# Regrouping the small matmuls between two recurrence chains of a hybrid attention and RWKV-7 step

## The chip, the cores and the metric

The kernel runs on one core of a Trainium2 chip. Its time is the device time of one execution in microseconds (us); the number that counts is the median over the timed runs. Engines are called as the profile calls them: PE (TensorE matmul), PEld (TensorE weight load), DVE (VectorE), ACT (ScalarE), POOL (GpSimd) and SP (SyncE, which issues the DMAs).

## What is computed

One inference step of a two-layer trunk of width 2048, for 512 latent tokens and 128 context tokens together (640 columns). Layer 0 is attention (differential heads and latent-compressed heads). Layer 1 is RWKV-7 time mixing: 32 heads of 64, one scan forward and one backward over the tokens. Each layer has a modulated norm before it and a gated residual behind it. The part that matters here is the scan of layer 1:

```python
def step(s, inp):
    r_t, w_t, k_t, v_t, kk_t, a_t = inp
    sa = jnp.einsum('bhij,bhj->bhi', s, -kk_t)
    s = s * w_t[:, :, None, :] + sa[..., None] * (kk_t * a_t)[:, :, None, :] + v_t[..., None] * k_t[:, :, None, :]
    return s, jnp.einsum('bhij,bhj->bhi', s, r_t)
```

and the modulation that comes before each norm, `m = silu(cond) @ w + b`, whose weight is 2048 x 6144 per layer.

## The kernel before, in words

All large products are done as three fp32r matmuls (high x high, high x low, low x high part; `project_steps`, L126), 320 columns each, with 128x512 weight tiles that come by DMA (`raw`), are rounded by ACT (`whi`) and subtracted by POOL (`wlo`). In the profile these are the `pj` matmuls (`part` and `first` at the start of the program).

The start of layer 0 (the first 160 us) computes the modulation: `adaln` (L171) reads 128x512 weight tiles (`araw`, 256 KB each) and multiplies them with four 32-column tiles of PE in turn (k = 0, 1, 2, 3, 0, ...; L176). It is a generator that stops after every k; the main code there (JOBS, JW) runs some of its steps, then one job of projection matmuls, and so on, for four blocks b. The order of PE is set by the scheduler there.

Layer 1's scan is done in chunks of 64 tokens. The work is cut in 32 units: 16 tiles of two heads, each in two halves u of five chunks per direction. For each unit the state-independent part is made first: decay and keys (`stage_a1`, `stage_e`: tiles AR and BK), the Gram matrices (`stage_a2`, L1114), the inverse of a unit triangular 64x64 matrix per chunk and head (`stage_a3` on DVE for 16x16 blocks, then `stage_inv` on PE for the rest), transposed keys (`stage_bk`, L1182), transposed values (`stage_pre`, `pvt`, L1202) and a product of Gram matrix and values (`pmv`, L1218). Then `stage_c` runs the chain over five chunks, each step needing the one before, and `stage_gn` normalises its output and transposes it (`pgn`, L1410).

`stage_inv` has four stages on PE with 32x32 tiles of the array, called the first to the fourth stage here: L1243 (result read by DVE at L1246), L1252 (read by DVE at L1257, two transposes, and by ACT at L1259, four copies), L1265 (read by ACT at L1268) and L1272 (read by ACT at L1275). All write the PSUM tile CC. The first two go round four tiles on the diagonal of the array from one matmul to the next. The last two do 20 matmuls on one tile, and then 20 on another.

Inside the scan the order of PE is the order in which the code issues it (`manual_schedule`); each other engine's order is set by the scheduler. `unit(n)` first interleaves the chain of unit n with the plan (P1), then, between this chain and the next, works off the list P2: pairs of a stage and a weight; a step of the stage is issued, and then `fill(weight)` issues projection matmuls from the plan of all coming projections, scaled so that they are spread evenly over the units. What a generator does up to its next `yield` stands on PE in one piece. PSUM tiles of the tag `pg` (two buffers) serve the transposes, `pmv`, and the Gram matrices.

Of the kernel before, what the change touches and what calls it, by code (L numbers as in the profile page):

```python
# [14 lines left out]
AF = mybir.ActivationFunctionType  # L15
# [6 lines left out]
KT = 16  # L22
HT = 320
WC = 512
NCH = 10
# [28 lines left out]
def kernel(  # L54
# [116 lines left out]
    def adaln(layer, psp, tag, sb, sc, blocks, bufs):  # L171
        for n in blocks:
            ps = psp.tile([128, 512], F32, tag=tag, name="ada")
            for k in range(KT):
                j = 32 * (k % 4)
                pe.matmul(ps[j:j + 32, :], sc[:, k, :], ada_raw(layer, n, k, sb, bufs), start=(k < 4),  # L176
                          stop=(k >= 12), tile_position=(0, j))
                yield
            row = sb.tile([128, T], F32, tag="tmp", name="row")[:, 0:512]
            act.activation(out=row, in_=ps, func=AF.Copy)  # L180
            pt = psp.tile([128, 512], F32, tag=tag, name="adat")
            for j in range(4):
                pe.transpose(pt[:, j * 128:(j + 1) * 128], row[:, j * 128:(j + 1) * 128], ident)
            ada_end(layer, n, pt.rearrange("p (j g r) -> p j r g", j=4, g=4)[:, :, 0:2, :], 4)
# [59 lines left out]
    with tc.tile_pool(name="x0", bufs=1, side="right") as xp0, \  # L244
# [42 lines left out]
                else:  # L287
                    dve.tensor_tensor(out=acc if out is None else out, in0=acc, in1=X, op=ALU.add)

        JOBS, JW = (0, 4, 1, 5, 2, 3), (None, (5, 5, 5, 5, 5, 5), (5, 5, 5, 5, 5, 5), (5, 6, 7, 8, 6, 0))  # L290
        for b in range(4):
            ga = adaln(0, pm, "pm", xt0, sc, (b, 4 + b), 8)
            if b:
                for i, job in enumerate(JOBS):
                    for _ in range(JW[b][i]):
                        next(ga, None)
                    if job < 4:
                        part(job, b - 1, None)
                    else:
                        chunk(fg[job - 4])  # L300
            for _ in ga:
                pass
            for k in range(4 * b, 4 * b + 4):
                modulate(x0[:, k, :], 0, k, h0hi, h0lo, xt0)
# [533 lines left out]
    with ExitStack() as l1:  # L838
# [336 lines left out]
        def stage_bk(i, u):  # L1175
            un = units[(i, u)]
            BKn = un.BKn = u1.tile([128, NCH, 128], F32, tag="BKn", name="BKn")
            for c in range(0, NCH, 4):
                n = min(4, NCH - c)
                ps = pg_tile("pbk")  # L1180
                for j in range(n):
                    pe.transpose(ps[:, j * 128:(j + 1) * 128], un.BK[:, c + j, :, :].rearrange("p a t -> p (a t)"), ident)  # L1182
                act.activation(out=BKn[:, c:c + n, :].rearrange("p c d -> p (c d)"), in_=ps[:, 0:n * 128], func=AF.Copy)
                yield

        def stage_v(i, u):
            t, un = tiles_[i], units[(i, u)]
# [7 lines left out]
        def stage_pre(i, u):  # L1195
            un = units[(i, u)]
            vv = un.vv
            UV = un.UV = u1.tile([128, NCH, 128], F32, tag="UV", name="UV")
            for c, n in ((0, 4), (4, 1)):
                ps = pg_tile("pvt")  # L1200
                for j in range(n):
                    pe.transpose(ps[:, j * 128:(j + 1) * 128], vv[:, c + j, :], ident)  # L1202
                for z in range(2):
                    o = 64 * (1 - z)
                    act.activation(out=UV[o:o + 64, un.ca[z] + c:un.ca[z] + c + n, :].rearrange("p c d -> p (c d)"),
                                   in_=ps[o:o + 64, 0:n * 128], func=AF.Copy)
                yield
            MV = un.MV = u1.tile([128, 5, 128], F32, tag="MV", name="MV")
            for s0, n in ((0, 4), (4, 1)):
                ps = pg_tile("pmv")  # L1210
                for s in range(s0, s0 + n):
                    for h in range(2):
                        hs = slice(64 * h, 64 * h + 64)
                        co = 128 * (s - s0) + 64 * h
                        for z in range(2):
                            cg = un.ca[z] + (4 - s if z else s)
                            o, ov = 64 * z, 64 * (1 - z)
                            pe.matmul(ps[o:o + 64, co:co + 64], un.GG[ov:ov + 64, cg, h, 0:64],  # L1218
                                      UV[ov:ov + 64, cg, hs], start=True, stop=True)
                act.activation(out=MV[:, s0:s0 + n, :].rearrange("p c d -> p (c d)"), in_=ps[:, 0:128 * n], func=AF.Copy)  # L1220
                yield

        def stage_inv(i, u):
            un = units[(i, u)]
# [30 lines left out]
            for o, col, q0 in grp:  # L1255
                if col == 0:
                    dve.transpose(out=b2(xn[o:o + 32]), in_=pa(o))  # L1257
            for o, col, q0 in grp:
                act.activation(out=b2(xd[o:o + 32, :, col:col + 32]), in_=pa(o), func=AF.Copy)  # L1259
            yield  # L1260
            t32 = xn
            for z, a, b, ca, cb in zh:
                o = 64 * z
                for q in range(10):
                    pe.matmul(blk(o + 32, q), G[o:o + 32, 2 * ca + q, 32:64], xn[o:o + 32, q, :],  # L1265
                              start=True, stop=True, tile_position=(o, o + 32))
            for o in (0, 64):
                act.activation(out=b2(t32[o + 32:o + 64]), in_=pa(o + 32), func=AF.Copy)  # L1268
            yield
            for o in (0, 64):  # L1270
                for q in range(10):
                    pe.matmul(blk(o, q), t32[o + 32:o + 64, q, :], xd[o + 32:o + 64, q, 32:64],  # L1272
                              start=True, stop=True, tile_position=(o + 32, o))
            for o in (0, 64):
# [111 lines left out]
        def stage_gn(i, u):  # L1386
# [20 lines left out]
            for s0, n in ((0, 4), (4, 1)):  # L1407
# [4 lines left out]
                for z in range(2):  # L1412
# [3 lines left out]
                        act.activation(out=y, in_=p4[:, :, z, :], func=AF.Copy)  # L1416
                    else:
                        dve.tensor_tensor(out=y, in0=y, in1=p4[:, :, z, :], op=ALU.add)
                yield

        def stage_bonus(i, u):
            if u:
# [59 lines left out]
                next(work[0], None)  # L1482

        CW = (3, 3, 2, 3)
        P2 = (('inv', 1), ('bk', 2), ('inv', 2), ('bk', 1), ('pre', 2), ('inv', 2), ('bonus', 1), ('bk', 1), ('inv', 2), ('pre', 2), ('bonus', 2), ('pre', 2), ('pre', 2), ('a2', 3), ('a2', 3), ('a2', 4))
        W2 = sum(w for _, w in P2)

        def step(g):
# [2 lines left out]
        def unit(n):  # L1491
# [5 lines left out]
            sub, a1, kk = of(stage_a3, n + 1), of(stage_a1, n + 2), kk_of(n + 2)  # L1497
            gn = stage_gn(*seq[n - 1]) if n else iter(())
            bonus, inv = of(stage_bonus, n), urgent(of(stage_inv, n + 1))
            P1 = {-1: [kk], 2: [gn, sub, kk], 4: [a1], 5: [kk, sub], 7: [a1], 8: [gn], 10: [a1], 11: [gn], 13: [a1], 15: [bonus]}  # L1500
            w1 = 0
            for g in P1[-1]:
                step(g)
# [25 lines left out]
        def prologue():  # L1529
# [10 lines left out]
                step(g)  # L1540
                fill(w)
            all_(a2, of(stage_a3, 0))
            for g, w in ((bk, 6), (bk, 6), (a1, 8), (bk, 6)):
                step(g)
                fill(w)
            all_(a1, bk)
# [1 line left out]
            all_(of(stage_e, 1))  # L1548
            of(stage_v, 0)
            script(dict(pre=of(stage_pre, 0), inv=urgent(of(stage_inv, 0)), a2=of(stage_a2, 1)),  # L1550
                   (("pre", 6), ("pre", 32), ("inv", 3), ("a2", 6), ("inv", 3), ("inv", 3),
                    ("a2", 6), ("pre", 3), ("inv", 3), ("pre", 3), ("a2", 6)))
            need(proj_r, 1)

        with tc.manual_schedule(engines={mybir.EngineType.PE}):
# [137 lines left out]
```

## Time and profile before

| | |
|---|---|
| median of 3 runs | 3726.73 us (3720.97 to 3733.14) |
| profiled execution | 3717.45 us, of which the span from the first to the last instruction is 3715.7 us |
| PE / DVE / ACT / POOL busy | 94% / 59% / 43% / 32% of the span |
| scan of layer 1 | from about 1640 us to about 3430 us |

Busy time of PE counts matmuls that overlap once. In a timeline row the first number is the start of the first of `x` instructions, the second the time to the end of the last; two rows that follow each other overlap, so that the cost of a group is read from its start to the start of the next row (its pitch). An fp32 matmul is two instructions in the trace and one in the order of the program, an fp32r matmul is one in both.

### The profile page before, as it was taken

To read this page: it belongs to the slowest core of one execution; us is meant where nothing else is said; L and a number is where in the kernel's file an instruction comes from. 1 tells how busy PE (TensorE), PEld (TensorE's weight loads), DVE (VectorE), ACT (ScalarE), POOL (GpSimd) and SP (SyncE) were. 2 spreads that over 40 slices of the span, in tenths; PEclk is the share of its full clock that TensorE was granted. 3 is DMA by queue.
4 is the path that set the end of the run, shared out by engine and by line. 5 is a ranking of instruction groups with operands and counts; after the bars stand their busy time and mean duration, and the time that the engine had idled before them with its cause. 6 is when DMAs were issued, how large, how long until landed. Compare 5 with 4: busy or idle time off the path is not lost. (4 is left out here: it accounts for less than half of the span.)

```text
span 3715.7 us, 83258 instructions
## 1 busy us (share of the span) xinstructions
PE 3491.8 (94%) x34176; PEld 3054.6 (82%) x34176; DVE 2183.1 (59%) x4232; ACT 1608.9 (43%) x3310; POOL 1189.5 (32%) x1094
## 2 busy tenths in 40 slices
PE   7999999999999989999999999999999999999998
PEld 3788889988888889887777787878878878787898
DVE  3355655666667564556666566666666666666402
ACT  2344443444444422544454444444444545445322
POOL 1222112222223344432333332323323333332444
PEclk9999999999999989999999999999999999999999
DMA  8723433333333464322222222222232222223534
GB/s 288 240 80 93 126 100 113 108 102 108 107 108 118 144 204 152 104 77 62 73 62 68 59 65 73 62 65 62 63 76 67 61 67 67 65 68 89 162 101 142
DMA packets 388462, 376.18 MB, mean 101 GB/s; under 512 B 200496, under 2 KB 242416, under 8 KB 388080
## 3 DMA queue, kind: packets, MB, share of 16 engines
q1 hardware_dynamic: 388080, 370.86, 34.3%
q8 instruction: 268, 4.39, 0.5%
q14 instruction: 114, 0.93, 0.1%
HBM read 328.51 MB, written 42.24 MB: 100 GB/s over the span
## 5 line engine op out<-in xcount | busy, mean ns | idle before, releaser
L101 POOL TENSOR_TENSOR wlo<-raw,whi 128x512 fp32r<-128x512 f32 (+1 forms) x628 | 854.4, 1361 | 2032.1 <-PE pj L126 1232.3
L126 PE MATMUL pj<-h0hi,wlo 128*128 128x320 f32 x4448 | 1091.2, 324 | 17.5 <-POOL wlo L101 17.3
L126 PE MATMUL pj<-h0hi,whi 128*128 128x320 f32 x4448 | 1089.2, 324 | 4.8 <-DVE gt L951 3.1
L126 PE MATMUL pj<-h0lo,whi 128*128 128x320 f32 x4448 | 1081.2, 322 | 1.1 <-POOL h0lo L101 0.8
L126 PEld LDWEIGHTS pj<-h0hi,wlo 128*128 128x128 f32 x4448 | 749.6, 192 | 51.9 <-POOL wlo L101 20.7
L126 PEld LDWEIGHTS pj<-h0hi,whi 128*128 128x128 f32 x4448 | 749.2, 192 | 38.3 <-issue 9.1
L126 PEld LDWEIGHTS pj<-h0lo,whi 128*128 128x128 f32 x4448 | 751.8, 191 | 29.2 <-issue 8.0
L100 ACT ACTIVATE whi<-raw 128x512 fp32r<-128x512 f32 (+1 forms) x628 | 390.5, 623 | 734.6 <-PE pj L126 444.0
L198 DVE SCALAR_TENSOR_TENSOR aacc<-araw,scs,aacc 128x512 f32<-128x512 f32 x480 | 401.7, 885 | 20.0 <-DMA araw<-in_dram 19.0
L362 DVE TENSOR_REDUCE nm<-S 128x1 f32<-128x768 f32 (+1 forms) x120 | 98.5, 821 | 257.6 <-PE S L374 257.5
L722 DVE SCALAR_TENSOR_TENSOR x<-pj,mod,xr 128x512 f32<-128x512 f32 (+2 forms) x68 | 33.3, 526 | 251.8 <-PE pj L126 246.1
L365 ACT ACTIVATE P<-S,nm 128x768 f32<-128x768 f32 (+1 forms) x120 | 95.2, 793 | 164.8 <-DVE nm L362 164.3
L1118 DVE TENSOR_TENSOR GG<-gram,con 128x512 f32<-128x512 f32 (+1 forms) x192 | 107.8, 597 | 79.6 <-PE gram L1114 79.5
L1303 ACT ACTIVATE Yn<-CC 128x128 f32<-128x128 f32 x160 | 44.4, 277 | 217.2 <-DVE rhs L1333 209.1
L1114 PE MATMUL gram<-AR,BK 64*128 64x128 f32 x1280 | 115.9, 295 | 20.8 <-DVE GG L1118 13.8
L1114 PEld LDWEIGHTS gram<-AR,BK 64*128 64x128 f32 x1280 | 91.8, 191 | 46.3 <-DVE GG L1118 24.1
L1348 DVE COPY UV<-CC 64x128 f32<-64x128 f32 x160 | 47.1, 295 | 130.6 <-ACT UV L1347 129.2
L1054 PE MATMUL plo<-lr,lw 96*128 96x320 f32 x256 | 104.1, 489 | 6.9 <-DMA lr<-lorad 6.6
L1347 ACT ACTIVATE UV<-CC 64x128 f32<-64x128 f32 x160 | 43.2, 270 | 148.0 <-PE CC L1345 147.4
L564 PE MATMUL po<-PT,vt 128*128 128x128 f32 x800 | 103.2, 276 | 0.1
L564 PEld LDWEIGHTS po<-PT,vt 128*128 128x128 f32 x800 | 98.0, 191 | 4.2 <-issue 2.5
L1056 ACT ACTIVATE tmp<-plo,vecs 128x320 f32<-128x320 f32 x128 | 67.5, 527 | 67.2 <-PE plo L1054 67.2
(338 smaller groups left out, 5306.3 us busy)
## 6 DMA issues: line engine op xcount, KB each, us to landing
raw<-in_dram SPq DMA_DIRECT2D x612, 256.0 KB
araw<-in_dram SPq DMA_DIRECT2D x384, 256.0 KB
lr<-lorad SPq DMA_DIRECT2D x128, 120.0 KB
Ld<-GG SPq DMA_DIRECT2D x64, 160.0 KB
lw<-in_dram SPq DMA_DIRECT2D x128, 48.0 KB
x<-in_dram SPq DMA_DIRECT2D x16, 320.0 KB
xr<-in_dram SPq DMA_DIRECT2D x16, 320.0 KB
DD<-Xd SPq DMA_DIRECT2D x32, 160.0 KB
```

The lines of the kernel that those rows point to most:

```text
L100: act.activation(out=hi, in_=src, func=AF.Copy)
L101: (lo_eng or pool).tensor_tensor(out=lo, in0=src, in1=rf(hi), op=ALU.subtract)
L126: pe.matmul(p[:n, 0:b - a], w, x[:, kk ^ flip, a:b], start=(kk == order[0] and i == 0), stop=(kk == order[-1] + kc - 1 and i == 2))
L198: dve.scalar_tensor_tensor(out=acc[:, s], in0=raw, scalar=scs[:, k, s:s + 1], in1=acc[:, s], op0=ALU.mult, op1=ALU.add)
L362: dve.tensor_reduce(out=nm, in_=S[:, 0:nk], axis=AX.X, op=ALU.max, negate=True)
L365: act.activation(out=P[:, 0:nk], in_=S[:, 0:nk], func=AF.Exp, bias=nm, accum_out=l)
L564: pe.matmul(po[:, 0:128], H.vt[:, kt, :], PT[:, j, :], start=(j == 0), stop=(j == n - 1))
L1054: pe.matmul(ps[:, 0:HT], lw, lo, start=True, stop=True)
L1056: act.activation(out=hv(tmp, z, ca, cb), in_=c3(ps[:, 0:HT]), func=AF.Exp, scale=-1.0, bias=nw0[:, bcol:bcol + 1])
L1114: pe.matmul(ps[:, j * 128:(j + 1) * 128], BK[hs, c + j, :, :].rearrange("p a t -> p (a t)"), AR[hs, c + j, :, :].rearrange("p a t -> p (a ...
L1118: dve.tensor_tensor(out=GG[:, c:c + n, h, :], in0=ps[:, 0:n * 128].rearrange("p (j t) -> p j t", t=128), in1=maskg.rearrange("p (o t) -> p ...
L1348: dve.tensor_copy(out=UV[64:128, cgs[1], :], in_=pu[1][64:128])
```

## The change

Five edits, all on the order of work; no instruction's shape is changed, and no arithmetic.

1. `stage_inv`: in the third and fourth stage the loop over q is outside and the loop over the two tiles inside. Of the four ACT copies behind the second stage (L1259) the two of the off-diagonal column stay; the other two (`xd[o:o+32, :, 0:32]`) are issued behind the third stage.
2. `stage_bk`, `stage_pre`, `stage_gn` yield less often: eight transposes and then two (before 4, 4, 2), five `pvt` (before 4, 1), twenty `pmv` matmuls (before 16, 4), five `pgn` (before 4, 1).
3. P2 puts each of these right behind a stage of the inverse with weight 0 between them; P1 loses one step of `gn`.
4. `adaln` makes four `araw` tiles, then issues four matmuls, then yields; it yields once more behind the ACT copy `row`. It has 12 buffers instead of 8.
5. JW and the weights of the prologue are adapted to the new number of steps.

```diff
-            for k in range(KT):
-                j = 32 * (k % 4)
-                pe.matmul(ps[j:j + 32, :], sc[:, k, :], ada_raw(layer, n, k, sb, bufs), start=(k < 4),
-                          stop=(k >= 12), tile_position=(0, j))
+            for g in range(0, KT, 4):
+                raws = [ada_raw(layer, n, g + j, sb, bufs) for j in range(4)]
+                for j, raw in enumerate(raws):
+                    pe.matmul(ps[32 * j:32 * j + 32, :], sc[:, g + j, :], raw, start=(g == 0),
+                              stop=(g == KT - 4), tile_position=(0, 32 * j))
                 yield
             row = sb.tile([128, T], F32, tag="tmp", name="row")[:, 0:512]
             act.activation(out=row, in_=ps, func=AF.Copy)
+            yield
...
-            ga = adaln(0, pm, "pm", xt0, sc, (b, 4 + b), 8)
+            ga = adaln(0, pm, "pm", xt0, sc, (b, 4 + b), 12)
...
-            for c in range(0, NCH, 4):
-                n = min(4, NCH - c)
+            for c, n in ((0, 4), (4, 4), (8, 2)):
                 ps = pg_tile("pbk")
...
-                yield
+                if c:
+                    yield
...
             for o, col, q0 in grp:
                 if col == 0:
                     dve.transpose(out=b2(xn[o:o + 32]), in_=pa(o))
-            for o, col, q0 in grp:
-                act.activation(out=b2(xd[o:o + 32, :, col:col + 32]), in_=pa(o), func=AF.Copy)
+                else:
+                    act.activation(out=b2(xd[o:o + 32, :, col:col + 32]), in_=pa(o), func=AF.Copy)
             yield
             t32 = xn
-            for z, a, b, ca, cb in zh:
-                o = 64 * z
-                for q in range(10):
+            for q in range(10):
+                for z, a, b, ca, cb in zh:
+                    o = 64 * z
                     pe.matmul(blk(o + 32, q), G[o:o + 32, 2 * ca + q, 32:64], xn[o:o + 32, q, :],
...
+            for o in (0, 64):
+                act.activation(out=b2(xd[o:o + 32, :, 0:32]), in_=pa(o), func=AF.Copy)
             yield
-            for o in (0, 64):
-                for q in range(10):
+            for q in range(10):
+                for o in (0, 64):
                     pe.matmul(blk(o, q), t32[o + 32:o + 64, q, :], xd[o + 32:o + 64, q, 32:64],
...
+        P2 = (('inv', 0), ('bk', 5), ('inv', 0), ('bk', 4), ('inv', 0), ('pre', 5), ('inv', 0), ('pre', 5), ('bonus', 1), ('bonus', 1), ('a2', 4),
+              ('a2', 4), ('a2', 4))
```

On PE, in the 22nd inverse of the program, from its second to its fourth stage, the order before was this (`pj` are projections, `pbn` a small sum over heads):

```order
L1252 MATMUL CC<-DD,t_14641 32x32 x40
L126 MATMUL pj<-h0hi,wlo 128x320 x2
L126 MATMUL pj<-h0hi,whi 128x320 x2
L126 MATMUL pj<-h0lo,whi 128x320 x2
L1182 MATMUL pbk<-con,BK 128x128 x4
L126 MATMUL pj<-h0hi,wlo 128x320 x2
L1202 MATMUL pvt<-con,vv 128x128 x4
L126 MATMUL pj<-h0hi,whi 128x320 x2
L126 MATMUL pj<-h0lo,whi 128x320 x2
L126 MATMUL pj<-h0hi,wlo 128x320 x2
L1265 MATMUL CC<-DD,GG 32x32 x20
```

and it is this now:

```order
L1254 MATMUL CC<-DD,t_14641 32x32 x40
L1183 MATMUL pbk<-con,BK 128x128 x2
L126 MATMUL pj<-h0lo,whi 128x320 x2
L126 MATMUL pj<-h0hi,wlo 128x320 x2
L126 MATMUL pj<-h0hi,whi 128x320 x2
L126 MATMUL pj<-h0lo,whi 128x320 x2
L126 MATMUL pj<-h0hi,wlo 128x320 x2
L1267 MATMUL CC<-DD,GG 32x32 x20
L1204 MATMUL pvt<-con,vv 128x128 x5
```

Between the second and the third stage there were seven pairs of `pj` and eight transposes; now there are five pairs and two transposes, and the `pvt` transposes follow the third stage. From the first stage to the second it goes from four transposes and four pairs to eight transposes and eight pairs; from the third to the fourth seven pairs follow the five `pvt`; behind the fourth the twenty `pmv` follow at once and then eight pairs, and up to the first Gram matrix there are 30 pairs of `pj` instead of 32.

On DVE, at the same place, the order before was this (`AR` and `BK` are made here for the unit after next):

```order
L1246 SCALAR_TENSOR_TENSOR t_14641<-CC,nlow,i_14637 128x5x16 x2
L1087 TENSOR_TENSOR AR<-kk,D 128x5x63
L1090 TENSOR_TENSOR AR<-rT,D 128x5x64
L1087 TENSOR_TENSOR AR<-kk,D 128x5x63
L1090 TENSOR_TENSOR AR<-rT,D 128x5x64
L1397 TENSOR_SCALAR gst<-gst 128x10
L1257 STREAM_TRANSPOSE DD<-CC 32x320 x2
```

and it is this now:

```order
L1248 SCALAR_TENSOR_TENSOR t_14641<-CC,nlow,i_14637 128x5x16 x2
L1089 TENSOR_TENSOR AR<-kk,D 128x5x63
L1092 TENSOR_TENSOR AR<-rT,D 128x5x64
L1089 TENSOR_TENSOR AR<-kk,D 128x5x63
L1092 TENSOR_TENSOR AR<-rT,D 128x5x64
L1259 STREAM_TRANSPOSE DD<-CC 32x320
L1085 TENSOR_TENSOR BK<-kk,az 128x5x64 x2
L1259 STREAM_TRANSPOSE DD<-CC 32x320
```

The two transposes behind the second stage stood together; now two products for BK stand between them. ACT's first copy (L1261) waits for the first transpose, the second transpose for that copy, and ACT's second copy for the second transpose.

## Rows read from the trace of the kernel before

**Rows 1.** The page: busy time of each engine, with share of the span and number of instructions.

```profile
PE 3491.8 (94%) x34176; PEld 3054.6 (82%) x34176; DVE 2183.1 (59%) x4232; ACT 1608.9 (43%) x3310; POOL 1189.5 (32%) x1094
```

**Rows 2.** Busy time by stretch: start and end, length, busy time of PE, PEld, DVE, ACT, POOL with the number of instructions, granted clock of PE, share of the DMA engines, GB/s. The first two are parts of the start, the third is the scan.

```profile
20.00:57.00 37.00, 28.32 (x99) 6.77 (x97) 18.36 (x31) 9.15 (x16) 0.05 (x1) 1.00 0.89 306
57.00:160.00 103.00, 100.80 (x595) 67.31 (x596) 20.44 (x43) 24.85 (x42) 26.66 (x21) 1.00 0.79 264
...
1640.00:3430.00 1790.00, 1678.92 (x22608) 1429.38 (x22608) 1160.39 (x2643) 853.59 (x1880) 567.07 (x630) 0.98 0.26 67
```

**Rows 3.** Whom PE waited for in the scan (1640 to 3430 us): us in total, times, longest.

```profile
PE CC L1265 <- ACT xd L1259: 27.2, 25, 2.6
PE CC L1345 <- ACT Yn L1303: 17.5, 37, 0.8
PE gram L1114 <- DVE GG L1118: 13.8, 18, 3.4
...
PE gram L1114 <- ACT MV L1220: 3.6, 11, 0.9
```

**Rows 4.** PE's timeline in the 22nd inverse, each stage with the row that follows it: start, length, engine, line, names, shapes, number of instructions, idle time before.

```profile
2839.72 0.86 PE L1243 MATMUL CC<-DD,GG 32*32 32x16 f32 x80
2840.51 0.56 PE L126 MATMUL pj<-h0lo,whi 128*128 128x320 f32 x2
...
2842.31 0.89 PE L1252 MATMUL CC<-DD,t 32*32 32x32 f32 x80
2843.13 0.56 PE L126 MATMUL pj<-h0hi,wlo 128*128 128x320 f32 x2
...
2846.84 1.35 PE L1265 MATMUL CC<-DD,GG 32*32 32x32 f32 x40 [0.51 <-ACT xd L1259]
2848.11 0.56 PE L126 MATMUL pj<-h0hi,whi 128*128 128x320 f32 x2
...
2850.79 1.35 PE L1272 MATMUL CC<-xd,DD 32*32 32x32 f32 x40
2852.07 0.56 PE L126 MATMUL pj<-h0hi,whi 128*128 128x320 f32 x2
2852.47 0.46 PE L126 MATMUL pj<-h0lo,whi 128*128 128x320 f32 x2
2852.76 0.46 PE L126 MATMUL pj<-h0hi,wlo 128*128 128x320 f32 x2
2853.06 0.27 PE L1202 MATMUL pvt<-con,vv 128*128 128x128 f32 x1
2853.08 0.54 PE L126 MATMUL pj<-h0hi,whi 128*128 128x320 f32 x2
2853.46 0.46 PE L126 MATMUL pj<-h0lo,whi 128*128 128x320 f32 x2
...
2854.92 0.46 PE L126 MATMUL pj<-h0hi,wlo 128*128 128x320 f32 x2
2855.31 1.15 PE L1218 MATMUL pmv<-UV,GG 64*64 64x64 f32 x32
2856.39 0.55 PE L126 MATMUL pj<-h0hi,whi 128*128 128x320 f32 x2
```

**Rows 5.** PE's timeline a little earlier, in the chain: four `pgn` transposes behind a 64-column group, with the two rows that follow.

```profile
2826.62 0.66 PE L1410 MATMUL pgn<-con,Yn 128*128 128x128 f32 x4
2827.04 0.54 PE L126 MATMUL pj<-h0lo,whi 128*128 128x320 f32 x2
2827.41 0.45 PE L126 MATMUL pj<-h0hi,wlo 128*128 128x320 f32 x2
```

**Rows 6.** The timelines of DVE and ACT behind the second stage of the 22nd inverse.

```profile
2843.89 1.05 DVE L1257 STREAM_TRANSPOSE DD<-CC 32x320 f32<-32x320 f32 x2
2845.03 1.75 ACT L1259 ACTIVATE xd<-CC 32x320 f32<-32x320 f32 x4 [2.49 <-DVE DD L1257]
```

**Rows 7.** Groups of instructions in the scan: line, engine, names, shapes, number | busy us, mean ns of one | idle time of the engine before them, and for whom.

```profile
L1083 DVE TENSOR_TENSOR BK<-kk,az 128x320 f32<-128x320 f32 x60 | 33.6, 599 | 74.1 <-PE pbk L1182 74.0
```

**Rows 8.** The timelines in the 21st inverse. On DVE a shift product of a projection and a pair of BK products that took longer than most; on ACT the copies of `pvt` to UV, two large and two small.

```profile
2789.84 0.75 DVE L889 SCALAR_TENSOR_TENSOR rT<-pj,vecs,rT 128x511 f32<-128x511 f32 x1 [1.20 <-ACT rT L887]
...
2795.56 1.96 DVE L1086 TENSOR_TENSOR BK<-BK,rate 128x320 f32<-128x320 f32 x2
...
2792.08 1.20 ACT L1205 ACTIVATE UV<-pvt 64x512 f32<-64x512 f32 x2
...
2797.52 0.56 ACT L1205 ACTIVATE UV<-pvt 64x128 f32<-64x128 f32 x2 [0.33 <-PE pvt L1202]
```

**Rows 9.** PE's timeline at the start, second block (b = 1) of the modulation: groups of ada matmuls of 2, 5 and 1 k, each with the row that follows.

```profile
61.41 1.05 PE L176 MATMUL ada<-araw,sc 128*32 128x512 f32 x4
62.39 0.56 PE L126 MATMUL first<-h0hi,whi 128*128 128x320 f32 x2
...
66.10 1.90 PE L176 MATMUL ada<-araw,sc 128*32 128x512 f32 x10
67.94 0.56 PE L126 MATMUL part<-h0hi,whi 128*128 128x320 f32 x2
...
71.65 1.04 PE L176 MATMUL ada<-araw,sc 128*32 128x512 f32 x2
72.63 0.56 PE L126 MATMUL first<-h0hi,whi 128*128 128x320 f32 x2
```

More of the change, by code (lines that the diff above doesn't have):

```diff
@@ L288, in part @@
                     dve.tensor_tensor(out=acc if out is None else out, in0=acc, in1=X, op=ALU.add)
-        JOBS, JW = (0, 4, 1, 5, 2, 3), (None, (5, 5, 5, 5, 5, 5), (5, 5, 5, 5, 5, 5), (5, 6, 7, 8, 6, 0))
+        JOBS, JW = (0, 4, 1, 5, 2, 3), (None, (2, 1, 2, 2, 1, 2), (2, 1, 2, 2, 1, 2), (2, 2, 1, 2, 3, 0))
         for b in range(4):
-            ga = adaln(0, pm, "pm", xt0, sc, (b, 4 + b), 8)
+            ga = adaln(0, pm, "pm", xt0, sc, (b, 4 + b), 12)
             if b:
@@ L1206, in stage_pre @@
                                    in_=ps[o:o + 64, 0:n * 128], func=AF.Copy)
-                yield
+            yield
             MV = un.MV = u1.tile([128, 5, 128], F32, tag="MV", name="MV")
@@ L1220, in stage_pre @@
                 act.activation(out=MV[:, s0:s0 + n, :].rearrange("p c d -> p (c d)"), in_=ps[:, 0:128 * n], func=AF.Copy)
-                yield
+            yield
         def stage_inv(i, u):
@@ L1418, in stage_gn @@
                         dve.tensor_tensor(out=y, in0=y, in1=p4[:, :, z, :], op=ALU.add)
-                yield
+            yield
         def stage_bonus(i, u):
@@ L1484 @@
         CW = (3, 3, 2, 3)
-        P2 = (('inv', 1), ('bk', 2), ('inv', 2), ('bk', 1), ('pre', 2), ('inv', 2), ('bonus', 1), ('bk', 1), ('inv', 2), ('pre', 2), ('bonus', 2), ('pre', 2), ('pre', 2), ('a2', 3), ('a2', 3), ('a2', 4))
+        P2 = (('inv', 0), ('bk', 5), ('inv', 0), ('bk', 4), ('inv', 0), ('pre', 5), ('inv', 0), ('pre', 5), ('bonus', 1), ('bonus', 1), ('a2', 4),
+              ('a2', 4), ('a2', 4))
         W2 = sum(w for _, w in P2)
@@ L1499, in unit @@
             bonus, inv = of(stage_bonus, n), urgent(of(stage_inv, n + 1))
-            P1 = {-1: [kk], 2: [gn, sub, kk], 4: [a1], 5: [kk, sub], 7: [a1], 8: [gn], 10: [a1], 11: [gn], 13: [a1], 15: [bonus]}
+            P1 = {-1: [kk], 2: [gn, sub, kk], 4: [a1], 5: [kk, sub], 7: [a1], 8: [gn], 10: [a1], 13: [a1], 15: [bonus]}
             w1 = 0
@@ L1542, in prologue @@
             all_(a2, of(stage_a3, 0))
-            for g, w in ((bk, 6), (bk, 6), (a1, 8), (bk, 6)):
+            for g, w in ((bk, 9), (a1, 8), (bk, 9)):
                 step(g)
@@ L1550, in prologue @@
             script(dict(pre=of(stage_pre, 0), inv=urgent(of(stage_inv, 0)), a2=of(stage_a2, 1)),
-                   (("pre", 6), ("pre", 32), ("inv", 3), ("a2", 6), ("inv", 3), ("inv", 3),
-                    ("a2", 6), ("pre", 3), ("inv", 3), ("pre", 3), ("a2", 6)))
+                   (("pre", 38), ("inv", 3), ("a2", 6), ("inv", 3), ("inv", 3),
+                    ("a2", 6), ("inv", 3), ("pre", 3), ("a2", 6)))
             need(proj_r, 1)
```

## Prediction

> **What bounds the kernel now.** The share of busy time comes first: PE is busy 94% of the span, no other engine over 59% [rows 1], so a stage can only get shorter where PE does less or waits less. The windows by stretch say where PE waits: in the scan it is busy 1678.9 of 1790 us, so 111 us are waits, a half of all its idle time; from 57 to 160 us, where the modulation is worked off between projections, only 2.2 us [rows 2]. The list of waits divides the 111 us: the largest entry, 27.2 us, is the third stage of the inverse waiting for ACT's four copies; 13.8 us are Gram matrices waiting for DVE to clear PSUM, 3.6 us for ACT's copy MV [rows 3]; most of the rest is inside the chain (17.5 us for Yn), which the change does not touch. The timeline, last, gives the cost of a group of PE as its pitch.
>
> **The inverse, third and fourth stage.** The reader is to see four stages with four pitches: 80 instructions in 0.79 us, 80 in 0.82, 40 in 1.27, 40 in 1.28 [rows 4]. So with four tiles in turn an instruction costs 10.3 ns (0.82/80), with one tile 31.8 and 32.0 ns. Two tiles in turn are not there with 32 columns. The nearest row is `pmv`, which alternates between two tiles with 64 columns: 32 instructions in 1.08 us, 33.8 ns [rows 4]; half the columns, so an estimate of 17 ns, or 0.68 us per stage. That takes off 0.59 and 0.60 us, 1.19 us per inverse, 38 us for 32 inverses. Bounds: 0 if two tiles don't overlap; 0.41 us per stage at 10.3 ns, that is 1.73 us per inverse or 55 us. I take 38, by the nearest row.
>
> A rule speaks against this. The third and fourth stages alternate between tiles in different rows of the array that write one PSUM bank; the second stage does the same with four tiles, and its rows show 10.3 ns against 31.8 for one tile [rows 4]. The Trainium skill (TensorEngine Tiling (Array Packing), Gotcha 1: PSUM Pressure) says that different row tiles cannot access the same PSUM bank simultaneously, so alternating would save nothing. By that rule the sum below would lose its 38 us; the trace disagrees for tiles that write different partitions.
>
> **Longer groups.** A pair of `pj` behind a pair costs 0.29 us (2852.47 to 2852.76); the first behind a matrix group 0.40 (2852.07 to 2852.47), so leaving a group costs 0.11; the last pair before one costs 0.39 (2854.92 to 2855.31), so entering costs 0.10 [rows 4]. For transposes it is otherwise. A single `pvt` takes 0.02 us and the pair behind it 0.38 (2853.08 to 2853.46), which is 0.11 together [rows 4]. Four `pgn` behind a 64-column group cost 0.42 and the pair behind them 0.37 [rows 5], 0.50 over the bare pair; four times 0.11 is 0.44. So transposes between projections cost only themselves, and behind a small-tile group 0.06 more, where leaving that group for `pj` would have cost 0.11. Each of the three transpose groups that now follow a stage saves 0.05 us: 0.15 per unit. `pmv` was two groups of its own, each with 0.10 + 0.11, behind a fourth stage that cost 0.11 to leave: 0.53. Now it costs 0.06 + 0.11: 0.36 saved. The lone `pgn` that joins its group costs 0.05, since its chain step is now left for `pj` directly. Together 0.46 us per unit, 14 us for 31. Bounds: 0, if the joint to the next group costs what leaving did, and 33 us, if each of six transpose groups saves 0.11 and each of two `pmv` groups 0.21 (1.08 us per unit).
>
> **The wait at the third stage.** It was 27.2 us over 32 inverses, 0.85 each [rows 3]. What covers it shrinks from seven pairs and eight transposes to five pairs and two transposes. Counted from the start of the second stage, PE now arrives after 0.82 + 0.06 + 2 x 0.11 + 5 x 0.29 + 0.10 = 2.65 us. On the other side: PE's last result 0.89, hand-over 0.05, first transpose 0.52 [rows 4, 6]; then DVE does the two BK products, 0.60 each [rows 7], before the second transpose (0.52); then 0.09 to ACT, one copy of 0.44 (1.75/4), 0.06 to PE [rows 6]. That is 3.77 us, a wait of 1.1 us: 0.25 more than before, 8 us in 31 units. So two ACT copies leave this path (0.88 us) and two DVE products enter it (1.20 us). That the BK products come so early is because `pbk` is done early: DVE waited 74.0 us for it [rows 7], idle time that cost PE nothing. Behind the transposes DVE has the rest of BK queued, for a Gram matrix some 8 us later. Bounds: no wait at all if the pair did not delay, 27 us gained; and if the pair takes 1.96 us and two shift products of 0.75 us get in front [rows 8], 2.26 us more, a wait of 3.4 us, 2.5 more than before, 78 us lost.
>
> **The new joint at `pmv`.** It needs all copies of `pvt`. From the start of the third stage ACT can start at 0.82, does four copies of 0.44 (two of them moved here), then 1.20 + 0.56 us for UV [rows 6, 8]: 4.3 us. PE reaches the fourth stage after 0.68 + 0.06 + 0.55 + 7 x 0.29 + 0.10 = 3.4 us, when its four copies are done (2.6), and `pmv` 0.74 us later, at 4.2. I take 0.2 us, 6 us in all; nothing if ACT starts at once, 0.8 us or 25 us if a weight or gate copy of about the size of those large ones gets in between. From the first to the second stage there are now eight transposes and eight pairs, over 3 us, and PE did not wait there with four and four [rows 4].
>
> **Gram matrices.** Some ten pairs (2.9 us) now lie between `pmv` and the first of them, so the 3.6 us for MV go. One pair more lies between two of them; 18 waits of 0.77 us on average lose 0.29 each, 5 us. Together 9 us, bounds 0 and 17.4 [rows 3].
>
> **The start.** Groups of ada matmuls do not cost in proportion: one k 0.98 us, two k 0.98, five k 1.84 [rows 9]. Four tiles run side by side, so a broken group pays for a full turn. The eight k of these three groups cost 3.80 us where two full turns would cost 1.96, 1.84 us less for a quarter of a block's 32 k. If half of each block is broken like that, three blocks give 11 us. But the DMA engines moved 264 GB/s there, and in the stretch before, where they were 89% busy, 306 [rows 2]; what is taken off here has to be made up by them, so I take about half, 6 us, bounds 0 and 12. The 12 buffers let SP issue more `araw` ahead; a weight tile queued behind them that comes late is in the lower bound.
>
> **The sum.** -38 - 14 + 8 + 6 - 9 - 6 = -53 us. Against its own execution, 3717.45 us, that gives 3664; the median of the runs lies 9 us higher, so 3674 is predicted for a median.
>
> **The rivals.** *Tiles in different rows exclude each other*: the 38 us are missing, 3712 us. The second stage speaks against it, but it has four tiles on the diagonal, and these two lie off it. *More than counted*: two tiles run at 10.3 ns (17 us more), groups are worth 33 us (19 more), the third stage no longer waits (35 more): 3603 us; for it speaks that DVE's order is freed of 74 us of waiting, against it the BK pair between the transposes. *The chain takes it back*: the DVE and ACT work per unit is the same in a shorter unit, and DVE's long products get in front of the chain's short ones; if half of the 47 us of the scan return as waits there, 3698 us. For it speaks that Yn alone waits 17.5 us [rows 3]; against it that DVE is busy 65% of the scan [rows 2]. *Slower*: the second transpose behind the BK products, with every unit as bad as [rows 8] has it, costs 78 instead of 8 us, 3744 us; it decides from a wait of 2.8 us per unit on (1.1 + 53/31). Against it: the mean of the product is 0.60 us. That the change does not do what it says is excluded by the order of PE.
>
> **How the numbers follow.** Forecast 0.55, with a range of its own of 3645 to 3700; row tiles exclude each other 0.10; more 0.15; chain 0.10; slower 0.10. A measurement of this kernel tells about 0.3%, 11 us, from no change: under 3715.5 is faster, over 3738 slower. Faster: the forecast, more, nearly all of the chain, and half of the first rival, 0.84; same: the rest of these and a part of the last, 0.07; slower 0.09. The range reaches from half-way into *more* (3625) to the first rival (3712).
>
> **What would show it.** Right: a pitch of about 0.7 us at the third and fourth stage; no `pj` between them and `pvt` and `pmv`; waits of PE for ACT's `xd` of 28 to 40 us in all; a small new wait of `pmv` for UV; none for MV; ada groups of 0.98 us each. Wrong: pitches of 1.27 us (first rival), or the third stage's wait over 85 us (slower), or growing waits of the chain for Yn, UV and S.

## The result, and the profile after

The median is 3683.93 us (3680.98 to 3687.32, 4 runs) against 3727.71 us of before, 44 us faster; the ratio of the runs is 0.990 with a 95% interval of 0.988 to 0.992, which is 37 us. 3674 us was predicted. The profiled execution has a span of 3679.2 us, 36.5 us less than before; the rows below divide those.

The page after, and the stretches of the start and the scan, from the first inverse's first stage to the last one's (columns as in [rows 2]):

```profile
PE 3428.9 (93%) x34176; PEld 3014.2 (82%) x34176; DVE 2185.6 (59%) x4232; ACT 1596.4 (43%) x3310; POOL 1176.4 (32%) x1094
...
20.00:57.00 37.00, 33.20 (x132) 11.14 (x132) 18.46 (x32) 10.39 (x17) 4.89 (x4) 1.00 1.03 376
57.00:160.00 103.00, 97.97 (x630) 71.84 (x629) 28.66 (x55) 29.48 (x49) 25.95 (x21) 1.00 0.75 248
1626.40:3376.70 1750.30, 1609.63 (x22273) 1376.23 (x22273) 1152.03 (x2630) 830.75 (x1858) 549.86 (x626) 0.98 0.27 68
```

The same stretch of the scan before:

```profile
1642.70:3415.10 1772.40, 1661.32 (x22281) 1412.92 (x22284) 1153.79 (x2630) 843.63 (x1858) 561.88 (x626) 0.98 0.26 67
```

PE is busy 51.7 us less in the scan, but the scan is only 22.1 us shorter: PE's waits in it grew from 111.1 to 140.7 us. The scan starts 16.3 us earlier (1642.7 to 1626.4), 12.7 of these won before the first attention score (237.4 to 224.7 us). The end behind the scan is 1.9 us longer. When the first score comes scatters by some 3 us: in the six profiled executions with the start of after (after itself and, below, `e2_transposes_first`, `e3_bonus_early`, `e5_both`, `e6_cover_moved` and `e7_no_cycle`) it came between 224.6 and 227.8 us.

The list of PE's waits in the scan after (1624 to 3414 us), which answers to [rows 3]:

```profile
PE CC L1267 <- ACT xd L1261: 59.6, 32, 4.4
PE pbn L1017 <- POOL hl L101: 13.9, 16, 1.7
PE CC L1349 <- ACT Yn L1307: 13.7, 35, 1.0
...
PE pbn L1017 <- ACT hl L100: 5.3, 14, 1.0
...
PE gram L1116 <- DVE GG L1120: 2.6, 4, 2.1
PE pmv L1220 <- ACT UV L1207: 1.5, 4, 0.7
```

The third stage's wait is not 27 us but 60; `pbn`, which did not stand in the list before, waits 19.2 us; the Gram matrices wait 11 us less for GG and no longer for MV. The waits of the chain did not grow (Yn 17.5 to 13.7).

PE's timeline after in the 22nd inverse, from its third stage to the first Gram matrix (columns as in [rows 4]):

```profile
2820.46 0.82 PE L1267 MATMUL CC<-DD,GG 32*32 32x32 f32 x40 [0.93 <-ACT xd L1261]
2821.21 0.77 PE L1204 MATMUL pvt<-con,vv 128*128 128x128 f32 x5
2821.74 0.54 PE L126 MATMUL pj<-h0hi,whi 128*128 128x320 f32 x2
...
2823.97 0.82 PE L1276 MATMUL CC<-xd,DD 32*32 32x32 f32 x40
2824.72 0.33 PE L1220 MATMUL pmv<-UV,GG 64*64 64x64 f32 x2
...
2829.55 0.45 PE L1017 MATMUL pbn<-hl,blkr 128*128 128x320 f32 x2
2829.83 0.45 PE L126 MATMUL pj<-h0hi,whi 128*128 128x320 f32 x2
2830.56 0.41 PE L1017 MATMUL pbn<-hl,blkr 128*128 128x320 f32 x1 [0.27 <-ACT hl L100]
2831.71 0.42 PE L1017 MATMUL pbn<-hl,blkr 128*128 128x320 f32 x1 [0.74 <-POOL hl L101]
```

Third and fourth stage have a pitch of 0.75 us each. The two `pbn` groups are one `pj` pair apart; the second needs a split (ACT's copy, POOL's difference) that is issued only behind the first.

The longest wait of the third stage, one unit earlier: PE, then DVE, then ACT.

```profile
2765.55 1.27 PE L1267 MATMUL CC<-DD,GG 32*32 32x32 f32 x40 [4.40 <-ACT xd L1261]
2766.75 1.33 PE L1204 MATMUL pvt<-con,vv 128*128 128x128 f32 x5
...
2768.41 0.73 PE L126 MATMUL pj<-h0lo,whi 128*128 128x320 f32 x2
2768.94 0.74 PE L126 MATMUL pj<-h0hi,wlo 128*128 128x320 f32 x2
```

```profile
2758.64 1.56 DVE L1092 TENSOR_TENSOR AR<-rT,D 128x320 f32<-128x320 f32 x1
2761.86 0.75 DVE L891 SCALAR_TENSOR_TENSOR rT<-pj,vecs,rT 128x511 f32<-128x511 f32 x1 [1.66 <-ACT rT L889]
2762.53 0.49 DVE L1259 STREAM_TRANSPOSE DD<-CC 32x320 f32<-32x320 f32 x1
2762.96 1.52 DVE L1085 TENSOR_TENSOR BK<-kk,az 128x320 f32<-128x320 f32 x2
2764.52 0.51 DVE L1259 STREAM_TRANSPOSE DD<-CC 32x320 f32<-32x320 f32 x1
```

```profile
2763.06 0.43 ACT L1261 ACTIVATE xd<-CC 32x320 f32<-32x320 f32 x1
2765.06 0.43 ACT L1261 ACTIVATE xd<-CC 32x320 f32<-32x320 f32 x1 [1.58 <-DVE DD L1259]
```

The second stage's last result was there at 2759.02, but DVE was on an AR product until 2760.20, and had a shift product for `rT` queued ahead of the first transpose, for which it waited for ACT's copy `rT`; then came the BK pair, 1.52 us, ahead of the second. Behind the 4.40 us PE runs at the lower of its two clock levels (granted clock 0.50): the stage has a pitch of 1.20 instead of 0.75 us, a `pj` pair 0.53 instead of 0.29. A wait can cost more than its length.

### The profile page after: what moved, and what is told of

Its sections match the earlier page's. It is cut to its first block, busy times and chain, and to the rows that moved or that the text cites. A ratio compares the mean times of both kernels' runs of the same rounds, so it can differ in the third digit from the quotient of the medians.

```text
span 3679.2 us, 83188 instructions
## 1 busy us (share of the span) xinstructions
PE 3428.9 (93%) x34176; PEld 3014.2 (82%) x34176; DVE 2185.6 (59%) x4232; ACT 1596.4 (43%) x3310; POOL 1176.4 (32%) x1094
## 5 line engine op out<-in xcount | busy, mean ns | idle before, releaser
L126 PEld LDWEIGHTS pj<-h0hi,whi 128*128 128x128 f32 x4448 | 754.2, 192 | 36.5 <-issue 8.7
L200 DVE SCALAR_TENSOR_TENSOR aacc<-araw,scs,aacc 128x512 f32<-128x512 f32 x480 | 409.5, 901 | 17.0 <-DMA araw<-in_dram 15.5
L1116 PE MATMUL gram<-AR,BK 64*128 64x128 f32 x1280 | 106.4, 292 | 5.8 <-DVE GG L1120 2.6
```

Source lines behind the costliest of these rows:

```text
L126: pe.matmul(p[:n, 0:b - a], w, x[:, kk ^ flip, a:b], start=(kk == order[0] and i == 0), stop=(kk == order[-1] + kc - 1 and i == 2))
L200: dve.scalar_tensor_tensor(out=acc[:, s], in0=raw, scalar=scs[:, k, s:s + 1], in1=acc[:, s], op0=ALU.mult, op1=ALU.add)
L1116: pe.matmul(ps[:, j * 128:(j + 1) * 128], BK[hs, c + j, :, :].rearrange("p a t -> p (a t)"), AR[hs, c + j, :, :].rearrange("p a t -> p (a ...
```

## Experiments

Waits and busy times of the runs are read from the same two views over each run's scan. Ratios are to the kernel before, with 95% intervals; the median of before lay between 3718 and 3728 us in the sets of executions that they go back to, so a difference of medians between two runs can be off by some us.

**Alternate tiles alone, in the kernel before** (`e1_cycle_only`):

```diff
-            for z, a, b, ca, cb in zh:
-                o = 64 * z
-                for q in range(10):
+            for q in range(10):
+                for z, a, b, ca, cb in zh:
+                    o = 64 * z
...
-            for o in (0, 64):
-                for q in range(10):
+            for q in range(10):
+                for o in (0, 64):
```

> The kernel before with one edit: the third and fourth stage of the inverse alternate between their two tiles. Theory: these stages take 0.75 us each as in the changed kernel (29.6 and 26.6 us busy instead of 44.1 and 46.0), nothing gives it back, and the time falls by 30 to 38 us, to 3690 to 3698 us; the wait at the third stage stays near 27 us. Rival (the chain takes it back): the stages are as short, but waits of the chain (Yn, UV, S) grow and the time stays above 3708 us.

Measured: 3698.84 us, 0.9935 (0.9911 to 0.9959), 24 us by the ratio, less than the 30 to 38 expected. The scan, with the columns of [rows 2]:

```profile
1634.90:3392.50 1757.60, 1631.47 (x22277) 1381.73 (x22277) 1154.74 (x2629) 839.46 (x1858) 563.92 (x626) 0.98 0.27 67
```

PE is busy 30 us less in the scan, and waits 15 us more (MV 3.6 to 11.2, GG 13.8 to 15.0, Yn 17.5 to 20.5). The stages take 0.75 us each also here, so the two tiles overlap; whether it is their matmuls or their weight loads that do, no run separates. "Nothing gives it back" was wrong: about half of what is saved in the scan comes back as waits, the most of it for MV, as if the Gram matrices came too early for ACT's copy.

**The start of before in the kernel after** (`e4_old_start`): loop, JW and 8 buffers of `adaln` as before.

```diff
-            for g in range(0, KT, 4):
-                raws = [ada_raw(layer, n, g + j, sb, bufs) for j in range(4)]
...
+            for k in range(KT):
+                j = 32 * (k % 4)
...
-            ga = adaln(0, pm, "pm", xt0, sc, (b, 4 + b), 12)
+            ga = adaln(0, pm, "pm", xt0, sc, (b, 4 + b), 8)
```

> The changed kernel with the modulation of before (one matmul per step, 8 buffers, old job weights). Theory (the start is worth what the traces show at the first attention score, 12 to 13 us, and the scan no more than 23): the time rises by 11 to 16 us, to about 3697 us. Rival (the start is worth the 6 us of the prediction and the rest is scatter between executions): 3690 us.

Measured: 3695.96 us, 0.9932 (0.9905 to 0.9958); first attention score at 236.9 us. The start is worth some 12 us. The scan:

```profile
1639.10:3392.30 1753.20, 1611.47 (x22273) 1377.14 (x22273) 1156.19 (x2630) 831.19 (x1858) 552.88 (x626) 0.98 0.27 67
```

What is left differs from `e1_cycle_only` by the new groups (with the copies and the prologue that go with them), and the two ratios agree within their intervals: with alternate tiles, the groups brought nothing in sum. PE is busy 20 us less in the scan than in `e1_cycle_only` (1631.5 to 1611.5) and waits 16 us more (126.1 to 141.7). The ratios split the whole 37 us into 24 for alternate tiles, 1 for the groups and 11 for the start.

**The groups alone** (`e9_group_only`): as `e4_old_start`, and the third and fourth stage in the order of before.

> Before with the new groups between the two chains alone: no alternate row tiles, and the start as before. Theory (the groups by themselves lose what the run without alternation lost over the scan, 1772.4 to 1793.7 us, and the start gains nothing here): 21 us slower than before, about 3740 us, with 59 us of waits ahead of the third stage. Rival (the groups gain the 9 us that the blind sum gave them, and the run without alternation was slow for another reason): about 3712 us.

Measured: 3740.15 us, 1.0051 (1.0031 to 1.0071), 19 us slower by the ratio, with 59.7 us of waits ahead of the third stage, as expected. The scan:

```profile
1637.00:3432.30 1795.30, 1659.17 (x22273) 1426.29 (x22273) 1146.66 (x2630) 832.72 (x1858) 547.54 (x626) 0.96 0.26 66
```

**The kernel after without alternate tiles** (`e7_no_cycle`, the first diff the other way round):

> After with the third and fourth inverse stage's instructions in the order of before (all of one row tile, then all of the other), everything else kept. Theory (alternate row tiles overlap, and the stages are on the path): 32 us from the sum of the two stages' shorter busy time, so about 3716 us; a part may come back since longer stages leave other chains more time, so 3700 to 3718. Rival (the regrouping brings the whole gain, alternation nothing): 3684 us.

Measured: 3724.13 us, 1.0011 (1.0001 to 1.0022), 40 us over after. The theory gave 3718 us at most. The scan is 43 us longer than in after, though PE waits 4 us less in it: the two stages are 36 us of that, and PE is busy 11 us longer with the rest of its work, at a granted clock of 0.97 in the scan against 0.98. The third stage's waits are alike in both (some 60 us), what follows is not. A wait of 1.22 us in this run, the rows behind it, and the granted clock of the stage and of the projections behind it:

```profile
2505.82 1.35 PE L1267 MATMUL CC<-DD,GG 32*32 32x32 f32 x40 [1.22 <-ACT xd L1261]
2507.10 0.90 PE L1204 MATMUL pvt<-con,vv 128*128 128x128 f32 x5
...
2508.33 0.73 PE L126 MATMUL pj<-h0hi,whi 128*128 128x320 f32 x2
2508.86 0.73 PE L126 MATMUL pj<-h0lo,whi 128*128 128x320 f32 x2
...
2505.90:2507.00 1.10, 1.10 (x40) 1.10 (x40) 1.07 (x4) 0.00 (x0) 0.00 (x0) 1.00 0.00 0
2507.10:2510.90 3.80, 3.80 (x20) 3.80 (x18) 1.14 (x3) 3.62 (x9) 1.28 (x1) 0.56 0.02 4
```

and the same stage of the same inverse in after, behind the same wait:

```profile
2480.77 0.82 PE L1267 MATMUL CC<-DD,GG 32*32 32x32 f32 x40 [1.22 <-ACT xd L1261]
2481.52 0.77 PE L1204 MATMUL pvt<-con,vv 128*128 128x128 f32 x5
...
2482.42 0.46 PE L126 MATMUL pj<-h0hi,whi 128*128 128x320 f32 x2
2482.71 0.46 PE L126 MATMUL pj<-h0lo,whi 128*128 128x320 f32 x2
...
2481.50:2485.30 3.80, 3.80 (x67) 3.56 (x61) 1.70 (x4) 3.58 (x9) 1.64 (x1) 1.00 0.01 4
```

Counted over the 32 inverses, three or more `pj` pairs within 6 us of the third stage's start run at the low level in 22 inverses without alternation (21 in `e9_group_only`), in 9 with it (7 in `e4_old_start`); in before, where the stage is the long one but the waits are short, in 2. In the whole scan the `pj` pairs with a pitch of 0.45 to 0.6 us cost, over 0.29 each, 55 us in both runs without alternation, 43 in after and 37 in before.

**DVE's transposes ahead of ACT's copies, in after** (`e2_transposes_first`):

```diff
             for o, col, q0 in grp:
                 if col == 0:
                     dve.transpose(out=b2(xn[o:o + 32]), in_=pa(o))
-                else:
+            for o, col, q0 in grp:
+                if col:
                     act.activation(out=b2(xd[o:o + 32, :, col:col + 32]), in_=pa(o), func=AF.Copy)
```

> The changed kernel with both DVE transposes behind the second stage issued ahead of ACT's two copies, so that no BK product stands between them. Theory (the BK products between the transposes are what the third stage waits for): its wait falls from 59.6 to under 35 us, and the time by 25 to 40 us, to 3644 to 3659 us. Rival (the wait comes from the shorter cover, five pairs instead of seven and eight transposes, or from ACT being busy): the wait stays over 45 us and the time over 3670 us.

Measured: 3651.84 us, 0.9802 (0.9776 to 0.9828). The wait falls from 59.6 to 35.0 us, in two rows:

```profile
PE CC L1268 <- ACT xd L1262: 27.5, 28, 2.4
...
PE CC L1268 <- DVE BK L1085: 7.5, 3, 3.4
```

So what stood between the transposes made 24.6 of the 32.4 us by which this wait had grown. The edit takes two things away there: the BK pair, and the second transpose's wait for ACT's first copy. The last inverse of after has no BK pair:

```profile
3381.50 0.51 DVE L1259 STREAM_TRANSPOSE DD<-CC 32x320 f32<-32x320 f32 x1 [3.37 <-PE CC L1254]
3382.74 0.50 DVE L1259 STREAM_TRANSPOSE DD<-CC 32x320 f32<-32x320 f32 x1 [0.72 <-ACT xd L1261]
```

Here the second transpose starts 1.24 us after the first, against 1.97 on average over the 32 inverses, and 0.52 in this run: by this one inverse, the BK pair costs some 0.7 us beyond the wait for the copy. The scan of the profiled execution is 36.7 us shorter, 24.6 by this wait; PE's busy time fell by 11.5 as well, with a clock of 0.984 (after 0.980). By the medians the edit brought 32 us.

**The two bonus groups apart** (`e3_bonus_early`):

```diff
-        P2 = (('inv', 0), ('bk', 5), ('inv', 0), ('bk', 4), ('inv', 0), ('pre', 5), ('inv', 0), ('pre', 5), ('bonus', 1), ('bonus', 1), ('a2', 4),
+        P2 = (('inv', 0), ('bk', 4), ('bonus', 1), ('inv', 0), ('bk', 4), ('inv', 0), ('pre', 5), ('inv', 0), ('pre', 5), ('bonus', 2), ('a2', 4),
```

> The changed kernel with the first of the two bonus steps moved up, behind the first transposes of the keys (bk 4, bonus 1, and bonus 2 before the Gram matrices). Theory: pbn no longer waits for its split (13.9 us for POOL and 5.3 us for ACT in the changed kernel) and the time falls by 15 to 20 us, to about 3666 us. Rival (the Gram matrices behind it then wait for BK or PSUM instead): the pbn wait goes, another takes its place, time within 5 us of 3684.

Measured: 3655.35 us, 0.9813 (0.9785 to 0.984), 29 us under after by the medians and more than the 15 to 20 expected. No wait for `hl` is left in the list, and UV in the chain waits 17.5 us instead of 10.9. The 64 `pbn` instructions fall from 20.5 to 14.6 us of busy time, as much as before: one that starts behind a wait is busy for 0.41 us (2830.56 and 2831.71 above), one in a row adds 0.15 (half the 0.29 of a pair).

**Both** (`e5_both`):

> After with both earlier edits together: VectorE's transposes ahead of ScalarE's two copies, and the two bonus groups apart. Theory (the two waits are separate chains: the copy of xd ahead of the third inverse stage, the split's second half ahead of pbn): the two gains add, 3683.9 - 32.1 - 28.6 = about 3623 us, with under 40 us of waits ahead of the third stage and none ahead of pbn. Rival (both take cover from the same pmv and pj work, so that one wait grows where the other goes): over 3640 us, third-stage wait again near 60 us.

Measured: 3628.28 us, 0.9757 (0.9742 to 0.9771), faster than both kernels: 92 us under before and 56 under after. The page has PE busy less and a larger share of the span:

```profile
PE 3409.7 (94%) x34176; PEld 3003.9 (83%) x34176; DVE 2202.5 (61%) x4232; ACT 1598.0 (44%) x3310; POOL 1195.6 (33%) x1094
```

The third stage waits 29.7 + 8.1 us, `pbn` not at all. The gains add for the most part: by the medians 56 of 61 us, by the ratios 54 of 70. The waits for UV (17.1) and GG (7.3) took a part.

**Most cover ahead of the third stage** (`e6_cover_moved`), in the kernel with both:

```diff
-        P2 = (('inv', 0), ('bk', 4), ('bonus', 1), ('inv', 0), ('bk', 4), ('inv', 0), ('pre', 5), ('inv', 0), ('pre', 5), ('bonus', 2), ('a2', 4),
-              ('a2', 4), ('a2', 4))
+        P2 = (('inv', 0), ('bk', 2), ('bonus', 1), ('inv', 0), ('bk', 8), ('inv', 0), ('pre', 5), ('inv', 0), ('pre', 4), ('bonus', 2), ('a2', 4),
+              ('a2', 4), ('a2', 3))
```

> As the run with both edits, and one more regrouping: most of the eight pj pairs that stood behind the third stage stand between the second and the third stage, eleven in all there. Theory (the wait ahead of the third stage is a fixed chain of about 2 us of VectorE and ScalarE work, which is covered by as much PE work as stands there): that wait falls to under 10 us in all and the time to about 3600 us. Rival (the work is only taken from another chain's cover): waits of the same size ahead of the fourth stage, pmv or the Gram products, and the time stays within 10 us of the run with both edits.

The expectation has it wrong where the cover is taken from. Per inverse, the pairs of `pj` between second and third stage rise from 5.6 to 11.4; they come from those between first and second (7.1 to 4.1) and those ahead of the first Gram matrix (10.0 to 8.6), while those behind the third stage stay (7.3 to 7.1).

Measured: 3639.21 us, 0.9783 (0.9769 to 0.9798), 11 us slower than with both, against some 28 faster expected. The wait did go, and others came:

```profile
PE CC L1350 <- ACT Yn L1308: 24.0, 48, 1.1
...
PE gram L1116 <- DVE GG L1120: 10.6, 9, 3.1
PE pmv L1220 <- ACT UV L1207: 10.0, 18, 1.4
PE CC L1268 <- ACT xd L1262: 7.0, 10, 1.2
```

With both, these four were 16.7, 7.3, 1.6 and 29.7. The rival is right that the wait only moves: PE waits 108 us of the scan with both and 106 here. Projections are a fixed stock of cover; the theory forgot that they covered others before. Why `pmv` waits longer, with as many pairs ahead of it, no run here shows. The loss of 11 us is not in the sum of the waits: in the profiled executions PE is busy 7 us longer in the scan (`pmv`, which now starts behind waits, goes from 46.7 to 51.4, the Gram matrices from 103.0 to 107.1), and the end behind the scan is 3 us longer.

**The start: 8 buffers in after** (`e8_bufs8`) **and 12 in before** (`e10_before_bufs12`), one number each:

> After with eight buffers for the rows of a instead of twelve, everything else of the start kept. Theory (the transfers of the start wait for free buffers, not for DMA engines): bytes between 20 and 57 us fall from 376 GB/s back to about 306 and the first attention score comes at about 235 us instead of 224.7. Rival (the other order of the start's loop and groups brings it): first score stays at about 225 us, GB/s near 376.

> Before with twelve buffers for the rows of a instead of eight, the loop and the groups of the start as they were. Theory (free buffers alone set the start's transfers): GB/s between 20 and 57 us rises from 306 to about 376, first attention score at about 225 us instead of 237, time about 12 us less than before. Rival (buffers only help with the new order of the loop): first score after 232 us, time within 6 us of before.

Measured: with 8 buffers in after 3688.01 us (one run), first score at 237.6; with 12 in before 3711.45 us, 0.9981 (0.9961 to 1.0002), which is not told from no change, first score at 230.2. The stretch from 20 to 57 us in the one and in the other:

```profile
20.00:57.00 37.00, 31.01 (x111) 8.80 (x110) 17.54 (x30) 9.32 (x16) 2.96 (x3) 1.00 0.98 338
```

```profile
20.00:57.00 37.00, 32.19 (x119) 11.60 (x119) 17.88 (x31) 10.32 (x18) 4.05 (x3) 0.95 1.05 379
```

Twelve buffers bring the 376 GB/s with either loop (369 to 379 in the seven executions that have them), eight do not (306 to 338 in five; 306 in before is the lowest). But the first score comes as early as in after only with both: 237.4 (neither), 237.6 (new loop), 230.2 (buffers), 224.7 (both), and PE's busy time in ada matmuls goes alike: 60.5, 62.5, 56.4, 53.1 us. Over all executions, neither gives 235.1 to 237.4 and both 224.6 to 227.8, so the buffers alone bring more than half, and the loop brings the rest only on top of them. Each theory of the two expectations held a half: the transfers wait for buffers, and with the old loop PE still takes what has come in groups of 2, 5 and 1 k.

## Why the prediction was right

The time lies in the forecast's own range, and two of the reasons named are shown, alternate tiles (24 us) and the start (11 to 12). The regrouping, which had -9 us in the sum with its waits, brought nothing in sum: two waits in the scan were missed, and part of that was made good by terms that brought more than was counted. That the total came out within 10 us is in part luck. One of its readings of the kernel before needs two more rows: DVE in the 22nd inverse, between PE's last result of the second stage (2843.20) and the first transpose (2843.89 [rows 6]).

```profile
2843.29 0.48 DVE L1090 TENSOR_TENSOR AR<-rT,D 128x320 f32<-128x320 f32 x1
2843.69 0.17 DVE L1397 TENSOR_SCALAR gst<-gst 128x10 f32<-128x10 f32 x1
```

By its terms:

- *Third and fourth stage, -38.* Right: 0.75 us each in place of 1.27 and 1.28, 1.05 us per inverse, 34 us. The estimate of 17 ns per instruction was 18.8 (0.75/40). The first rival is refuted. The rule of the Trainium skill that stood behind it (TensorEngine Tiling (Array Packing), Gotcha 1: PSUM Pressure), that different row tiles cannot access the same PSUM bank at the same time, would have left the stage at 1.27 us; for these two tiles, which write different partitions of one bank, the trace disagrees with 0.75.
- *Longer groups, -14.* Near in size: PE's busy time in the scan fell by 51.7 us, 33.9 of them in the two stages (44.1 + 46.0 to 29.6 + 26.6), which leaves 17.8, after `pbn` cost 5.9 more behind its waits. Not borne out is the way to it: an alternated stage costs 0.75 us up to a `pj` pair (`e1_cycle_only`) as well as up to `pvt`, so the 0.05 per joint is not there.
- *Wait at the third stage, +8.* This step failed: it was +32. The mechanism is the one named, a chain of DVE and ACT work with the BK pair between the transposes (`e2_transposes_first`), but the chain was sized too short at its beginning: 0.05 us were put down from PE's last result to the first transpose. The rows that it cites show 0.69 in that inverse (2842.31 + 0.89 to 2843.89 [rows 4, 6]), because DVE was still on the AR products that stand ahead of the transposes in its order. Over the 32 inverses it is 0.81 us in before and 0.77 in after; 0.05 is what it takes where DVE is free. From the start of one transpose to that of the other it takes 1.97 us instead of 0.52 + 1.20, and PE arrives after 2.86 instead of 2.65. Together 0.72 + 0.25 - 0.21 = 0.76 us on top of 1.1: the 1.86 us (59.6/32) that were measured. In all, 59.6 us lie between the sign of being right (28 to 40) and the sign of *slower* (over 85).
- *`pmv`, +6.* 1.5 us, and 1.8 us of waits for vT went: nothing.
- *Gram matrices, -9.* GG -11.2, MV -3.6, BK +0.6: -14.
- *Start, -6.* -12.7. The step that halved it, DMA engines that would have to make up the rest, was wrong: 89% busy by the profile, they moved 306 GB/s, and 376 as soon as there were more free buffers. PE's ada matmuls fell by 7.4 us (60.5 to 53.1); what the sum did not have is that PE also waits 4.9 us less between 20 and 57 us (28.3 to 33.2 busy).
- *Not in the sum:* the two bonus steps back to back. They cost 19.2 us of waits, and `e3_bonus_early` gave back 29. The prediction read the new P2 for `bk`, `pre` and `pmv` and did not ask what the second bonus step waits for.

So the busy time in the scan came out at the predicted figure (-52 against -51.7), in part by luck, since the two stages brought less and the rest more, and the waits did not: +5 against +30. The scan gave 22 us where 47 were counted; the start gave 7 more than counted, and the medians lie 7 us further apart than the two profiled executions. The fourth rival's mechanism was at work at 1.86 us per unit, under the 2.8 from which it would have decided. The third rival is refuted for after (Yn, UV and S did not grow), though `e1_cycle_only` shows a part of it: PE waits 5 us longer for Yn and UV there, and 9 for MV and GG; in `e6_cover_moved` it waits 24.0 us for Yn.

## What to carry to other kernels

Small matmuls that write different partitions were worth alternating between tiles here, even two, and more so with the longer waits of the new groups ahead of them. Where projections serve as cover, list for each group that is moved or joined what its next step waits for, and count in that chain what stands ahead of its first step in the engine's order. Add the chain up for the kernel before first: with 0.05 us the terms give 3.89 us from the second stage's start to the third's, and the rows show 4.53. Keep two steps of a generator that hand work to other engines apart, and issue the work of the later consumer (here the BK pair) behind the chain that PE waits for.

## What was not expected of the hardware

The edits depend on each other, in part by PE's clock. Alternate tiles are worth 24 us in before (1 to 0.9935) and 44 us with the new groups (1.0051 to 0.9932); the groups cost 19 us without alternate tiles and nothing with them. In the scan, alternation takes 14.8 us off before and 42.1 us off the kernel with the groups. Of these 27 us more, 18 are busy time of PE (30 against 48 us less) and 9 are waits: in before 15 us came back as waits, with the groups 6. With the groups, the wait at the third stage is the same with and without alternation; behind it a stage of 1.28 us on one tile at a time was followed by the low clock level in 22 and 21 of 32 inverses, a stage of 0.75 us on two tiles in 9 and 7. Why one is followed by it and the other not, no run here shows, and how much of the 18 us the clock makes is not measured by itself. In one execution a us of wait removed brought more than a us: in `e2_transposes_first` 24.6 us less of one wait went with a scan shorter by 36.7 us; the medians, 32 us apart, say less.
